# A decoder layer on one core: keys ahead of the query rotation, two units ahead of the scan, products in another order, residual in the accumulators, last tile by chunks

## The chip, the core and the metric

The kernel runs on one core of a Trainium2 chip. The core has TensorE (PE, the matmuls; PEld is its weight load), VectorE (DVE), ScalarE (ACT), GpSimd (POOL) and SyncE (SP), on whose queue nearly all DMAs are issued. The metric is the device time of one execution in microseconds (us), lower is better, as a median of runs.

## The reference

One step of a hybrid decoder layer in fp32: sliding-window attention with sinks and a Mamba-2 scan, both from one input projection and gated into one residual, then a squared-ReLU MLP. 1024 prompt positions and 8 single decode tokens go through the same weights (the kernel holds them as 1032 columns, T). Model width 1024, 16 query heads and 4 key heads of 64, window 128, 32 scan heads of 64 in 4 groups with a state of 128, MLP width 4096.

```python
def hybrid_layer(x, pos, ...):
    h = rms_norm(x, norm_mix)
    q, k, v, z, xbc, dt_raw, gates = jnp.split(h @ w_in, IN_SPLITS, axis=-1)
    q = rope(rms_norm(q.reshape(b, t, N_HEADS, HEAD_DIM), q_norm), pos)
    k = rope(rms_norm(k.reshape(b, t, KV_HEADS, HEAD_DIM), k_norm), pos)
    ...
    xc, conv_state = causal_conv(xbc, conv_prev, conv_w, conv_b)
    xs, Bm, Cm = jnp.split(xc, ...)
    y, h_fin = ssd_scan(xs_h, dt, A, Bm, Cm, ssm_h0)
    y = (y + d_skip[:, None] * xs_h).reshape(b, t, D_INNER)
    o_ssm = rms_norm(y * jax.nn.silu(z), ssm_norm)
    g_attn, g_ssm = jnp.split(jax.nn.sigmoid(gates), 2, axis=-1)
    mixed = g_attn * (o_attn @ w_attn_o) + g_ssm * (o_ssm @ w_ssm_o)
    x = x + mixed @ w_out
    u = rms_norm(x, norm_mlp) @ w_up
    x = x + jnp.square(jax.nn.relu(u)) @ w_down
    return x, new_k, new_v, conv_state, h_fin
```

## The kernel before

Activations lie with features on the partitions and the 1032 positions along the free side, in chunks (CH) of 384, 384 and 264 columns. Each fp32 matrix is kept as a high and a low fp32r part: `split` (L134) is a copy on ACT (L135) and a subtraction on DVE (L136). A product is three matmuls per 128 rows of K, high by high, high by low, low by high (`mm3`, L154).

**The stages.** Norm of the input and keys and values, until about 95 us; attention, mixed with matmuls of the input projection for other outputs, until 430; the scan, mixed with more of them, until 1080; output projections and the gate, until 1460; the MLP's up product, until 1827; its down product, until the end.

**Units.** Work of the input projection that something else can be laid over stands in a list of jobs, one for each 128 output columns. `unit` (L212) takes one chunk of a job: 24 matmuls and the eviction from PSUM. A conv job (L613) is three units; when its third is evicted, ACT makes the first tap (L629), DVE three more (L632 and L633 for each), ACT a Silu (L634), and the tile is an operand of the scan.

**Order.** From L838 to L1251 PE runs its instructions in the order of the code; within L840 to L852 ACT and DVE do too. Elsewhere a list scheduler orders each engine's queue.

**Attention's start.** L841 and L842 scale the rotary tables, `q_unit` (L692) makes a query tile and loads its shifted copy sw by DMA, `q_rot` (L709) rotates it on DVE and POOL and splits it into E and Od, `q_norm` (L729) makes its scales, `k_tiles` (L676) transposes the keys ktm (written at L443) on PE and splits them into KHH (ACT) and KLL (DVE). The scores (sc, L766) need E, Od, KHH and KLL.

**The scan.** Four groups g of eight chunks c. `front` (L1078) makes the decay matrix w (ACT), transposes B and x on PE (L1099) and scales them; `back` (L1112) makes state and output; its results go through yt (L1140) on DVE. `decode_unit` (L1036) is the decode token's part, without PE. PSUM for this comes from `bank` (L1075). 18 units run ahead of group 0 (L1154); then n of them are spread over the eight chunks of a group, half of a chunk's ahead of its back (L1171 to L1179).

**MLP up.** Each pair of 128x128 blocks is made by a scheme of seven products with sums of weight blocks and of input blocks (L1556 to L1610) for 16 pairs m. The first two products of the first eight m are made earlier and stored (p1). `prod` (L1412) is 12 matmuls of 258 columns, twice for a product (s = 0, 1). X and Y are two pairs of PSUM banks; u2, u3 and c21 are sums on DVE. `pair_loads` (L1548) loads the weights of the next m, `emit_u` (L1438) makes relu and square on ACT and writes u to DRAM. The inputs' sums are held in x23, x14 and x22 (L1495 to L1498).

**MLP down.** Eight passes e over the 4096 rows, each of four tiles of u that `load_ups` (L1537) loads by chunks (ld) and splits; within a pass eight output tiles n of three chunks, 12 matmuls each; DVE adds the sum into dacc (L1655). In pass 0 the other addend is the residual, loaded by chunk (xr, L1651). In the last pass `emit_y` (L1621) transposes tile n - 1 behind tile n, evicts it in two halves (yo, two buffers, L1629) and stores it; tile 7 comes last (L1659).

## Time and profile before

| | |
|---|---|
| median of 3 runs | 2214.3 us (2213.69 to 2218.34) |
| the profiled execution | 2215.28 us, its span 2213.5 us |
| busy: PE, DVE, ACT, POOL | 97%, 61%, 45%, 14% of the span |
| mean granted clock of PE | 0.992 of full speed |
| moved by DMA | 258.6 MB, mean 117 GB/s |

The profile is of one execution. Busy is the time in which an engine works on an instruction; the rest is waiting, for another engine, a DMA or nothing that the profile shows. The granted clock is 1 at 2.4 GHz and 0.5 at 1.2 GHz.

### The profile page before, as it was taken

How to read it: one execution, taken by the hardware profiler on the slowest of the kernel's cores; microseconds unless marked ns; L12 is line 12 of the kernel's file. 1: busy time of each engine (PE TensorE's matmuls, PEld its weight loads, DVE VectorE, ACT ScalarE, POOL GpSimd, SP SyncE). 2: the span in 40 equal slices, each digit the busy share in tenths (PEclk: the TensorE clock that was granted, in tenths of full speed). 3: DMA queues.
4: the chain of work that ended last, by engine and by line, in shares of the span. 5: the costliest groups of instructions: out<-in, count | busy, mean ns of one | idle time of the engine just before them, and what ended most of it. 6: DMA issues, size and time to landing. Idle time of an engine off the chain costs nothing.

```text
span 2213.5 us, 38986 instructions
## 1 busy us (share of the span) xinstructions
PE 2148.3 (97%) x14860; PEld 2045.0 (92%) x14860; DVE 1347.7 (61%) x2900; ACT 1006.4 (45%) x2040; POOL 318.7 (14%) x394
## 2 busy tenths in 40 slices
PE   7989999998999999999999999999999999999998
PEld 7989999997888898877999999999999998999998
DVE  6788787247756766677254867468665544544442
ACT  4265555235657656567353333336545542211112
POOL 1222222001213222223200003230000000000000
PEclk9999999999999999999999999999999999999999
DMA  5222233312324224133475766656443345332222
GB/s 189 81 77 67 74 101 91 98 54 64 91 68 127 61 80 122 42 84 103 117 228 175 237 195 190 185 169 190 139 120 101 113 129 176 111 100 87 86 71 79
DMA packets 341889, 258.64 MB, mean 117 GB/s; under 512 B 30864, under 2 KB 326503, under 8 KB 341661
## 3 DMA queue, kind: packets, MB, share of 16 engines
q1 hardware_dynamic: 340085, 254.87, 38.5%
q8 instruction: 117, 1.92, 0.4%
q10 hardware_dynamic: 1616, 1.28, 0.2%
q14 instruction: 71, 0.58, 0.1%
HBM read 180.26 MB, written 73.67 MB: 115 GB/s over the span
## 4 chain that ended last, share of the span: by engine, by line
PE 80%; DVE 9%; DMA 5%; ACT 4%; issue 2%; SPq 1%; POOL 0%; DVEq 0%; ACTq 0%; POOLq 0%
PE mm L158 14%; PE mm L159 14%; PE mm L160 14%; PE dn L158 5%; PE dn L160 5%; PE dn L159 5%; PE mm L1418 2%; PE mm L1419 2%; PE mm L1420 2%; PE dn L1418 2%; PE dn L1420 2%; PE dn L1419 2%; DMA bcb<-bc_d 2%; PE psy L1132 1%; PE psi L1125 1%
## 5 line engine op out<-in xcount | busy, mean ns | idle before, releaser
L158 PE MATMUL mm<-hT_h,wh 128*128 128x384 f32 (+1 forms) x1536 | 501.4, 326 | 1.1 <-ACT spill L239 1.1
L160 PE MATMUL mm<-hT_h,wl 128*128 128x384 f32 (+1 forms) x1536 | 492.1, 320 | 0.0
L159 PE MATMUL mm<-hT_l,wh 128*128 128x384 f32 (+1 forms) x1536 | 491.9, 320 | 0.0
L158 PEld LDWEIGHTS mm<-hT_h,wh 128*128 128x128 f32 x1536 | 290.3, 189 | 14.0 <-issue 12.1
L135 ACT ACTIVATE wh<-wraw 128x1024 fp32r<-128x1024 f32 (+1 forms) x157 | 160.3, 1023 | 296.5 <-PE dn L159 181.7
L159 PEld LDWEIGHTS mm<-hT_l,wh 128*128 128x128 f32 x1536 | 290.1, 189 | 0.0
L160 PEld LDWEIGHTS mm<-hT_h,wl 128*128 128x128 f32 x1536 | 289.6, 189 | 0.0
L158 PE MATMUL mm<-oh,wh 128*128 128x384 f32 (+2 forms) x832 | 257.2, 309 | 1.3 <-ACT pr L1306 1.1
L160 PE MATMUL mm<-oh,wl 128*128 128x384 f32 (+2 forms) x832 | 256.0, 308 | 1.4 <-DVE wl L136 1.4
L136 DVE TENSOR_TENSOR wl<-wraw,wh 128x1024 fp32r<-128x1024 f32 (+1 forms) x157 | 187.1, 1194 | 115.2 <-ACT wh L135 114.2
L159 PE MATMUL mm<-ol,wh 128*128 128x384 f32 (+2 forms) x832 | 256.8, 309 | 0.0
L1655 DVE TENSOR_TENSOR dacc<-dacc,dn 128x384 f32<-128x384 f32 x168 | 85.6, 510 | 150.4 <-PE dn L160 150.4
L158 PEld LDWEIGHTS mm<-oh,wh 128*128 128x128 f32 x832 | 156.6, 188 | 2.4 <-ACT pr L1306 1.5
L160 PEld LDWEIGHTS mm<-oh,wl 128*128 128x128 f32 x832 | 156.8, 188 | 1.6 <-DVE wl L136 1.6
L159 PEld LDWEIGHTS mm<-ol,wh 128*128 128x128 f32 x832 | 156.4, 188 | 0.0
L632 DVE SCALAR_TENSOR_TENSOR xc<-raw,prm,xc 128x1024 f32<-128x1024 f32 x72 | 93.5, 1299 | 7.0 <-ACT xc L629 6.9
L784 ACT ACTIVATE cm<-cm,nm,rq 128x128 f32<-128x128 f32 x128 | 61.7, 483 | 54.2 <-DVE nm L780 54.2
L1322 POOL TENSOR_TENSOR gr<-gr,rs 128x384 f32<-128x384 f32 (+1 forms) x24 | 29.2, 1218 | 272.1 <-ACT gr L1321 266.3
L1047 DVE SCALAR_TENSOR_TENSOR s<-s,dap,uu 128x128 f32<-128x128 f32 x128 | 47.5, 398 | 33.7 <-ACT uu L1046 33.6
L1046 ACT ACTIVATE uu<-bcb,dtp 128x128 f32<-128x128 f32 x128 | 42.4, 391 | 50.5 <-DMA bcb<-bc_d 49.5
L1284 DVE STREAM_TRANSPOSE xo<-xt 32x256 f32<-32x256 f32 x128 | 55.8, 436 | 8.1 <-DMA xT_d<-xo 3.9
L624 ACT ACTIVATE raw<-mm 128x384 f32<-128x384 f32 (+1 forms) x72 | 32.1, 447 | 60.6 <-PE mm L160 60.5
(821 smaller groups left out, 5366.8 us busy)
## 6 DMA issues: line engine op xcount, KB each, us to landing
wraw<-in_w_in SPq DMA_DIRECT2D x64, 512.0 KB
u_d<-u SPq DMA_DIRECT2D x64, 258.0 KB
wraw<-in_w_down SPq DMA_DIRECT2D x32, 512.0 KB
wraw<-in_w_up SPq DMA_DIRECT2D x27, 512.0 KB
ld<-u_d SPq DMA_DIRECT2D x56, 192.0 KB
xt<-in_x_prompt SPq DMA_DIRECT2D x16, 512.0 KB
s<-in_state_ssm SPq DMA_DIRECT2D x32, 256.0 KB
out_ssm_sample<-s SPq DMA_DIRECT2D x32, 256.0 KB
```

The source lines that it names most:

```text
L135: first = S.activation(h, src, AF.Copy)
L136: second[:] = [V.tensor_tensor(l, src, h.bitcast(F32), ALU.subtract)]
L158: TE.matmul(ps, lhsT=a, rhs=h, start=k == 0, stop=False)
L159: TE.matmul(ps, lhsT=a, rhs=l, start=False, stop=False)
L160: TE.matmul(ps, lhsT=b, rhs=h, start=False, stop=k == kt - 1)
L632: V.scalar_tensor_tensor(out[:, :NP], raw[:, k:k + NP], wk, out[:, :NP], ALU.mult, ALU.add)
L784: S.activation(cm[:, h, :], cm[:, h, :], AF.Exp, bias=nm[:, h:h + 1], scale=rq[:, j, h:h + 1], accum_out=sm[:, h:h + 1])
L1284: V.transpose(xo[32 * j:32 * j + 32, :, 32 * i:32 * i + 32], xb[32 * i:32 * i + 32, :, j, :])
L1418: TE.matmul(ps, lhsT=a, rhs=h, start=first and k == 0, stop=False, skip_group_check=True)
L1419: TE.matmul(ps, lhsT=a, rhs=l, start=False, stop=False, skip_group_check=True)
L1420: TE.matmul(ps, lhsT=b, rhs=h, start=False, stop=k == 3, skip_group_check=True)
L1655: V.tensor_tensor(ac[:, cs], prev, ps[:, :cn], ALU.add)
```

## The change

Five edits. (A) `k_tiles(0)` is called ahead of the first `q_rot` and not behind the second unit. (B) 20 units and not 18 stand ahead of the first scan, and 19, not 21, are spread over its group 0. (C) The seven products come in another order: into the banks X vt2, X vt3, Y vt1, X vt4, Y v22 before, and X vt2, Y vt1, X vt3, Y v22, X vt4 now; the pairs of input sums are placed in tiles accordingly. (D) The residual is loaded into the accumulators dacc by eight loads of a whole tile, `residual(n)`, four ahead of the first weights of pass 0 in the code and four behind; the chunk loads xr go, and all passes add alike. (E) `emit_y` can do a part of a tile; tile n - 1 is emitted behind the first chunk of tile n, and tile 7 by chunks of three, three and two blocks.

```diff
@@ -842,12 +842,12 @@
...
             q_unit(0, 0, 0)
             q_unit(0, 0, 1)
+            k_tiles(0)
             q_rot(0, 0, 0)
             unit(ahead=False)
             q_norm(0, 0)
             q_rot(0, 0, 1)
             unit(ahead=False)
-            k_tiles(0)
             unit(ahead=False)
             prefetch()
         blocks = [(kv, b) for kv in range(NKV) for b in range(NB)]
@@ -1151,7 +1151,7 @@
         rows(1)
...
-        unit(18)
+        unit(20)
         for g in range(NG):
...
@@ -1168,7 +1168,7 @@
...
-            n = (21, 27, 27, 9)[g]
+            n = (19, 27, 27, 9)[g]
...
@@ -1492,10 +1492,10 @@
     def xpair(i):
         return tuple(xv.tile([P, T], F32R, tag=f"x{i}{t}", name=f"x{i}{t}") for t in "hl")
 
-    x23 = [xpair(q) for q in range(4)]
-    x14 = [xpair(4 + q) for q in range(4)]
+    x21 = [xpair(q) for q in range(4)]
+    x34 = [xpair(4 + q) for q in range(4)]
     x22 = [tuple(xv.tile([P, HT], F32R, name=f"v{q}{t}") for t in "hl") for q in range(4)]
-    vt2, vt3, vt1, vt4, v22 = chunk_of(x23, 0), chunk_of(x23, HT), chunk_of(x14, 0), chunk_of(x14, HT), chunk_of(x22, 0)
+    vt2, vt1, vt3, vt4, v22 = chunk_of(x21, 0), chunk_of(x21, HT), chunk_of(x34, 0), chunk_of(x34, HT), chunk_of(x22, 0)
...
@@ -1513,24 +1513,24 @@
         V.tensor_tensor(b11_, b12_, b11_, ALU.subtract)
         t2 = mp.tile([P, HT], F32, tag="sa", name="t2")
...
-        split(x23[q][0][:, H0], x23[q][1][:, H0], t2)
+        split(x21[q][0][:, H0], x21[q][1][:, H0], t2)
...
     for q in range(4):
-        split(x23[q][0][:, H1], x23[q][1][:, H1], xrow[q][:, H1])
+        split(x21[q][0][:, H1], x21[q][1][:, H1], xrow[q][:, H0])
     early(5)
     wa[6] = w_first(6)
     for q in range(4):
-        split(x14[q][0][:, H0], x14[q][1][:, H0], xrow[q][:, H0])
+        split(x34[q][0][:, H0], x34[q][1][:, H0], xrow[q][:, H1])
     early(6)
     wa[7] = w_first(7)
     for q in range(4):
-        split(x14[q][0][:, H1], x14[q][1][:, H1], xrow[q + 4][:, H0])
+        split(x22[q][0][:], x22[q][1][:], xrow[q + 4][:, H1])
     early(7)
     for q in range(4):
-        split(x22[q][0][:], x22[q][1][:], xrow[q + 4][:, H1])
+        split(x34[q][0][:, H1], x34[q][1][:, H1], xrow[q + 4][:, H0])
 
...
@@ -1565,12 +1565,12 @@
         V.tensor_tensor(s2, s1, a11, ALU.subtract)
         w2, w3, w4 = wslot(), wslot(), wslot()
         split(w2[0][:, 0:4], w2[1][:, 0:4], s2)
+        split(w2[0][:, 4:8], w2[1][:, 4:8], s1)
         V.tensor_tensor(a21, a11, a21, ALU.subtract)
-        split(w2[0][:, 4:8], w2[1][:, 4:8], a21)
-        split(w3[0][:, 0:4], w3[1][:, 0:4], s1)
-        split(w3[0][:, 4:8], w3[1][:, 4:8], a22)
+        split(w3[0][:, 0:4], w3[1][:, 0:4], a21)
         V.tensor_tensor(a12, a12, s2, ALU.subtract)
-        split(w4[0][:, 0:4], w4[1][:, 0:4], a12)
+        split(w3[0][:, 4:8], w3[1][:, 4:8], a12)
+        split(w4[0][:, 0:4], w4[1][:, 0:4], a22)
 
...
@@ -1579,7 +1579,7 @@
         X = [bank(s) for s in range(2)]
         Y = [bank(s) for s in range(2)]
         pc = [p1[:, s * HC:(s + 1) * HC] for s in range(2)]
-        u2, u3 = [], []
+        u2, t5 = [], []
         for s in range(2):
             prod(X[s], w2, 0, vt2(s), True)
             u2.append(mp.tile([P, HC], F32, tag="u2", name="u2"))
@@ -1587,47 +1587,56 @@
         if m >= FP:
             second_product(m, w1, A)
         for s in range(2):
-            prod(X[s], w2, 4, vt3(s), False)
-            u3.append(mp.tile([P, HC], F32, tag="u3", name="u3"))
-            V.tensor_tensor(u3[s], X[s], pc[s], ALU.add)
+            prod(Y[s], w2, 4, vt1(s), True)
+            t5.append(mp.tile([P, HC], F32, tag="u3", name="t5"))
+            V.tensor_tensor(t5[s], Y[s], pc[s], ALU.add)
         if m == NM - 1:
             load_ups(0, lambda: p1t("ld"), HT)
         u = u_tile()
         for s in range(2):
-            prod(Y[s], w3, 0, vt1(s), True)
-            V.tensor_tensor(u3[s], u3[s], Y[s], ALU.add)
-            emit_u(2 * m + 1, 1, u, s, u3[s])
+            prod(X[s], w3, 0, vt3(s), False)
+            V.tensor_tensor(t5[s], X[s], t5[s], ALU.add)
+            emit_u(2 * m + 1, 1, u, s, t5[s])
         u = u_tile()
         for s in range(2):
-            prod(X[s], w3, 4, vt4(s), False)
+            prod(Y[s], w3, 4, v22(s), False)
+            V.tensor_tensor(u2[s], Y[s], u2[s], ALU.add)
+            emit_u(2 * m, 1, u, s, u2[s])
+        u = u_tile()
+        for s in range(2):
+            prod(X[s], w4, 0, vt4(s), False)
             c21 = mp.tile([P, HC], F32, tag="ca", name="c21")
             V.tensor_tensor(c21, X[s], pc[s], ALU.add)
             emit_u(2 * m + 1, 0, u, s, c21)
-        u = u_tile()
-        for s in range(2):
-            prod(Y[s], w4, 0, v22(s), False)
-            V.tensor_tensor(u2[s], u2[s], Y[s], ALU.add)
-            emit_u(2 * m, 1, u, s, u2[s])
     mst.close()
     lst.close()
 
 
     dap_ = ctx.enter_context(pool("dap", 1))
     yp = ctx.enter_context(pool("yp", 2))
-    accs = [dap_.tile([P, T], F32, name=f"dacc{n}") for n in range(8)]
+    accs = {n: dap_.tile([P, T], F32, name=f"dacc{n}") for n in (4, 5, 6, 7, 0, 1, 2, 3)}
+
+    def residual(n):
+        DQ.dma_start(accs[n], x2_d[n])
+
     FE = 4
     NE = 32 // FE
 
-    def emit_y(n):
+    def emit_y(n, c0=0, cn=T):
+
         ac = accs[n]
         ns = slice(n * P, (n + 1) * P)
+        b0, b1 = c0 // P, min((c0 + cn) // P, NB)
         ps = ptr.tile([P, NB, P], F32, tag="tr", name="psy2")
-        for tb in range(NB):
+        for tb in range(b0, b1):
             TE.transpose(ps[:, tb, :], ac[:, tb * P:(tb + 1) * P], ident)
-        for hf in range(2):
+        for t0 in range(b0, b1, 4):
+            t1 = min(t0 + 4, b1)
             yo = yp.tile([P, 4, P], F32, tag="yo", name="yo")
-            S.activation(yo, ps[:, 4 * hf:4 * hf + 4], AF.Copy)
-            DQ.dma_start(O["y_prompt"][0, 512 * hf:512 * hf + 512, ns].rearrange("(b p) n -> p b n", p=P), yo)
+            S.activation(yo[:, 0:t1 - t0], ps[:, t0:t1], AF.Copy)
+            DQ.dma_start(O["y_prompt"][0, t0 * P:t1 * P, ns].rearrange("(b p) n -> p b n", p=P), yo[:, 0:t1 - t0])
+        if c0 + cn < T:
+            return
         ps = pdn.tile([P, 512], F32, tag="dn", name="dnd")
         TE.transpose(ps[:ND, :P], ac[:, NP:T], ident)
         yd = yp.tile([ND, P], F32, tag="yd", name="yd")
@@ -1635,7 +1644,13 @@
         DQ.dma_start(O["y_sample"][:, 0, ns], yd)
 
     for e in range(NE):
+        if e == 0:
+            for n in range(4):
+                residual(n)
         w0 = load_w(w_dn, 0, k0=e * FE, kt=FE, ncol=256)
+        if e == 0:
+            for n in range(4, 8):
+                residual(n)
         if e + 1 < NE:
             load_ups(e + 1, lambda: yp.tile([P, 384], F32, tag="ld", name="ld", bufs=4), 384)
         uh = lambda k: ups[e][k][0]
@@ -1646,17 +1661,14 @@
                 ac = accs[n]
                 for c0, cn in CH:
                     cs = slice(c0, c0 + cn)
-                    if e == 0:
-                        xr = yp.tile([P, 384], F32, tag="xr", name="xr")
-                        DQ.dma_start(xr[:, :cn], x2_d[n, :, cs])
                     ps = pdn.tile([P, 512], F32, tag="dn", name="dn")
                     mm3(ps[:, :cn], wh, wl, uh, ul, FE, c0, cn, n0=(n % 2) * P)
-                    prev = xr[:, :cn] if e == 0 else ac[:, cs]
-                    V.tensor_tensor(ac[:, cs], prev, ps[:, :cn], ALU.add)
-                if e == NE - 1:
-                    if n:
-                        emit_y(n - 1)
-    emit_y(7)
+                    V.tensor_tensor(ac[:, cs], ac[:, cs], ps[:, :cn], ALU.add)
+                    if e == NE - 1:
+                        if n and c0 == 0:
+                            emit_y(n - 1)
+                        if n == 7:
+                            emit_y(n, c0, cn)
```

**A.** DVE's queue at the start of attention, both pieces of the difference in which KLL (L689) is named; L841 and L842 are the table scales, L714 and L716 the rotation.

```order
 L841 TENSOR_SCALAR cosq<-cosq,sml 128x1032
 L842 TENSOR_SCALAR sinq<-sinq,sml 128x1032
+L689 TENSOR_TENSOR KLL<-pk,KHH 64x512 x4
 L714 TENSOR_TENSOR q<-q,cosq 128x384
 L716 TENSOR_TENSOR q<-q,sw 128x384
```

```order
 L714 TENSOR_TENSOR q<-q,cosq 128x384
 L716 TENSOR_TENSOR q<-q,sw 128x384
-L689 TENSOR_TENSOR KLL<-pk,KHH 64x512 x4
 L136 TENSOR_TENSOR wl<-wraw,wh 128x1024
 L773 COPY_PREDICATED cm<-maski,sc 128x512
```

The four subtractions of KLL moved from behind both rotations to the place ahead of the first.

**B.** ACT's queue around the first front of the scan, before: L624 evicts a unit, L629 and L634 begin and end the last conv tile that the front reads, L1092 and L1093 make the decay matrix.

```order
L624 ACTIVATE raw<-mm 128x384
L135 ACTIVATE wh<-wraw 128x1024
L624 ACTIVATE raw<-mm 128x264
L1092 ACTIVATE w<-pdf 128x512
L629 ACTIVATE xc<-raw,prm 128x1032
L1092 ACTIVATE w<-pdf 128x512
L1104 ACTIVATE bt<-pcb 128x128
L1093 ACT_TABLE_LOAD
L1093 ACTIVATE w<-w 128x1024
L634 ACT_TABLE_LOAD
L634 ACTIVATE xc<-xc 128x1032
```

The same place now:

```order
L624 ACTIVATE raw<-mm 128x384
L135 ACTIVATE wh<-wraw 128x1024
L624 ACTIVATE raw<-mm 128x264
L629 ACTIVATE xc<-raw,prm 128x1032
L624 ACTIVATE raw<-mm 128x384
L634 ACTIVATE xc<-xc 128x1032
L624 ACTIVATE raw<-mm 128x384
L1092 ACTIVATE w<-pdf 128x512 x2
L1104 ACTIVATE bt<-pcb 128x128
L1093 ACT_TABLE_LOAD
L1093 ACTIVATE w<-w 128x1024
```

The evictions of two more units stand between the last conv tile's steps, and its Silu stands ahead of the front's work.

**D.** SP's queue from the end of MLP up into the down product, before: L1444 writes u, L1545 loads u (the 516 wide for pass 0, the 384 wide for pass 1), L1651 loads the residual by chunk, L143 loads weights.

```order
L1444 DMA u_d_76<-u_20322 128x516
L1545 DMA ld_20548<-u_d_76 128x384
L1545 DMA ld_20404<-u_d_76 128x516
L1545 DMA ld_20408<-u_d_76 128x516
L1545 DMA ld_20412<-u_d_76 128x516
L1545 DMA ld_20416<-u_d_76 128x516
L1545 DMA ld_20552<-u_d_76 128x384
L1545 DMA ld_20556<-u_d_76 128x384
L1545 DMA ld_20560<-u_d_76 128x384
L1651 DMA xr_20596<-x2_d_75 128x384
L1444 DMA u_d_76<-u_20420 128x516
L1651 DMA xr_20612<-x2_d_75 128x384
```

Now, from the second write of u on (four loads of 516 columns and the load of dacc0 stand between it and the write above it):

```order
L1444 DMA u_d_76<-u_20420 128x516
L1620 DMA dacc1_20531<-x2_d_75 128x1032
L1620 DMA dacc2_20532<-x2_d_75 128x1032
L1620 DMA dacc3_20533<-x2_d_75 128x1032
L1444 DMA u_d_76<-u_20452 128x516
L1444 DMA u_d_76<-u_20484 128x516
L1620 DMA dacc4_20526<-x2_d_75 128x1032
L1620 DMA dacc5_20527<-x2_d_75 128x1032
L1620 DMA dacc6_20528<-x2_d_75 128x1032
L1620 DMA dacc7_20529<-x2_d_75 128x1032
L1545 DMA ld_20556<-u_d_76 128x384
L1545 DMA ld_20560<-u_d_76 128x384
```

The first loads of u for pass 1 stood ahead of the second write of u, among the writes; they stand now behind the last write and behind all eight residual loads.

On DVE, the same place, now: L136 splits weights (wl) and u (x4l to x7l), L1666 adds into the accumulators (L1655 before).

```order
L136 TENSOR_TENSOR wl<-wraw,wh 128x1024
L1666 TENSOR_TENSOR dacc_20530<-dacc_20530,dn 128x384 x2
L1666 TENSOR_TENSOR dacc_20530<-dacc_20530,dn 128x264
L1666 TENSOR_TENSOR dacc_20531<-dacc_20531,dn 128x384 x2
L1666 TENSOR_TENSOR dacc_20531<-dacc_20531,dn 128x264
L136 TENSOR_TENSOR x4l<-ld,x4h 128x384
L136 TENSOR_TENSOR x5l<-ld,x5h 128x384
L1666 TENSOR_TENSOR dacc_20532<-dacc_20532,dn 128x384
```

The six adds of the first two tiles stand ahead of x4l; before, the first add stood behind x4l and x5l.

## Rows read from the trace of the kernel before

**Rows 1.** The page, busy us (share of the span) and instructions of each engine.

```profile
PE 2148.3 (97%) x14860; PEld 2045.0 (92%) x14860; DVE 1347.7 (61%) x2900; ACT 1006.4 (45%) x2040; POOL 318.7 (14%) x394
```

**Rows 2.** Who PE waited for: us in total, times, longest us.

```profile
PE pxt L1099 <- ACT xc L634: 6.7, 1, 6.7
...
PE mm L1418 <- DVE u L1586: 4.9, 4, 1.8
PE dn L158 <- DVE dacc L1655: 3.4, 1, 3.4
PE sc L766 <- ACT KHH L687: 2.9, 1, 2.9
PE pxt L1099 <- DVE yt L1140: 2.6, 1, 2.6
```

**Rows 3.** Stretches: length, busy PE PEld DVE ACT POOL, PEclk, DMA share, GB/s.

```profile
514.00:518.70 4.70, 0.00 (x1) 0.00 (x1) 4.57 (x7) 4.61 (x4) 1.07 (x2) 0.50 0.50 138
518.70:523.90 5.20, 5.20 (x17) 4.14 (x18) 4.18 (x15) 4.61 (x9) 1.53 (x3) 0.50 0.14 40
550.00:658.00 108.00, 103.74 (x687) 90.89 (x686) 72.39 (x170) 63.90 (x102) 20.29 (x31) 0.98 0.29 83
1540.00:1660.00 120.00, 113.11 (x932) 111.93 (x931) 75.87 (x153) 58.35 (x132) 0.00 (x0) 1.00 0.46 142
...
1826.00:1846.30 20.30, 15.16 (x95) 14.19 (x93) 12.98 (x24) 11.14 (x24) 0.00 (x0) 0.97 0.71 230
1832.00:1836.00 4.00, 4.00 (x28) 4.00 (x28) 2.62 (x5) 0.89 (x1) 0.00 (x0) 1.00 1.00 325
1846.30:1852.00 5.70, 5.70 (x21) 5.70 (x22) 1.39 (x3) 0.00 (x0) 0.00 (x0) 0.52 0.77 250
```

**Rows 4.** Timeline at attention's start, ACT, DVE, POOL: start, us, instruction [idle before <-releaser].

```profile
94.36 0.49 ACT L702 ACTIVATE q<-mm 128x384 f32<-128x384 f32 x1 [3.33 <-PE mm L160]
...
96.31 0.96 DVE L443 TENSOR_TENSOR ktm<-kb,rk 128x768 f32<-128x768 f32 x1
...
104.35 0.76 DVE L842 TENSOR_SCALAR sinq<-sinq,sml 128x1032 f32<-128x1032 f32 x1 [1.11 <-DMA sinq<-in_sin_fm]
...
106.75 0.56 DVE L716 TENSOR_TENSOR q<-q,sw 128x384 f32<-128x384 f32 x1 [0.91 <-POOL sw L715]
...
116.20 2.79 DVE L689 TENSOR_TENSOR KLL<-pk,KHH 64x512 fp32r<-64x512 f32 x4 [2.72 <-ACT KHH L687]
...
115.18 0.99 POOL L722 TENSOR_TENSOR Od<-q,Od 64x384 fp32r<-64x384 f32 x1
```

**Rows 5.** Timeline of ACT, the conv job before the last one.

```profile
499.94 0.37 ACT L624 ACTIVATE raw<-mm 128x264 f32<-128x264 f32 x1
...
505.89 1.07 ACT L634 ACTIVATE xc<-xc 128x1032 f32<-128x1032 f32 x1 [2.03 <-DVE xc L633]
```

**Rows 6.** The page's groups: count | busy us, mean ns | idle before, its releaser.

```profile
L632 DVE SCALAR_TENSOR_TENSOR xc<-raw,prm,xc 128x1024 f32<-128x1024 f32 x72 | 93.5, 1299 | 7.0 <-ACT xc L629 6.9
```

**Rows 7.** Timeline of DVE in MLP up.

```profile
1559.74 0.69 DVE L1564 TENSOR_TENSOR s<-wraw 128x512 f32<-128x512 f32 x1 [2.88 <-DMA wraw<-in_w_up]
```

**Rows 8.** Timeline of SP and DVE at the start of MLP down.

```profile
1831.14 0.32 SPq L1444 DMA_DIRECT2D u_d<-u  x1
...
1842.92 0.43 DVE L136 TENSOR_TENSOR x5l<-ld,x5h 128x264 fp32r<-128x264 f32 x1 [2.34 <-ACT x5h L135]
...
1845.70 0.88 DVE L1655 TENSOR_TENSOR dacc<-xr,dn 128x384 f32<-128x384 f32 x2
```

**Rows 9.** The page, what the DMAs moved in the whole span.

```profile
DMA packets 341889, 258.64 MB, mean 117 GB/s; under 512 B 30864, under 2 KB 326503, under 8 KB 341661
```

**Rows 10.** Timeline of ACT at the end.

```profile
2208.72 0.60 ACT L1629 ACTIVATE yo<-psy 128x512 f32<-128x512 f32 x1 [1.70 <-DMA out_y_prompt<-yo]
```

**Rows 11.** The chain that ended last, in order of time: start, us, what.

```profile
2202.52 0.18 PE dn L160
...
2204.57 0.12 PE dn L160
```

## Prediction

> **What bounds the kernel now.** I read the page's busy table first: TensorE (PE) is busy 2148.3 of 2213.5 us [rows 1], so the whole kernel is one PE queue with 65 us of holes in it, and an edit can win only holes and the slow-clock time behind them. Next the table of who PE waited for: the reader is to see five of its entries, each at a place that the change touches [rows 2]. They make 20.5 us. Then the stretches around those places with their granted clock [rows 3], because a hole is followed by matmuls at half clock. Last the timelines of DVE, ACT and SP ahead of each hole, for what ended last there [rows 4, 5, 7, 8]. PE runs the order that the code gives, so a hole closes only if other matmuls stand ahead of the wait, or what is waited for comes earlier. A matmul of 384 columns takes 0.18 us, one of 264 takes 0.12 [rows 11]; a unit of 24 takes 24 x 0.18 = 4.3 us.
>
> **A, keys ahead of the query rotation: about 1.5.** The scores waited 2.9 us for the key halves KHH [rows 2], since the key transposes stood behind two units. The last operand was KLL, done at 116.20 + 2.79 = 118.99 [rows 4]. Now the transposes come right behind the second query unit, which PE leaves when ACT starts to evict it, at 94.36. They read ktm, which DVE ends at 96.31 + 0.96 = 97.27: a new wait of up to 2.9 us, with the two units behind it. That wait falls ahead of the same scores, so it is not lost twice; what counts is when the scores have all operands. KLL's 2.79 us now stand on DVE between sinq (ends 105.11) and the first rotation multiply. They push the multiply from 105.28 to 107.90, by 2.6; the 0.91 that DVE waited there for POOL is covered by it, so the rotation chain comes 1.7 later, and its last product Od moves from 115.18 + 0.99 = 116.17 to 117.9 [rows 4]. The scores are then ready at 117.9 and not at 119.0: 1.1 gained, and something of the half-clock stretch behind the old hole. I take 1.5. Bounds: -1, if the rotation chain slips by all of 2.6 and the wait for ktm cools the clock, to +2.5, nearly the whole old wait.
>
> **B, two units more ahead of the first scan: about 10.** The hole of 6.7 us is the first transposes of the scan waiting for the Silu of the last conv tile [rows 2]. That tile's last unit stood directly ahead. The conv job before shows how long this takes: its eviction ends at 499.94 + 0.37 = 500.31 and its Silu at 505.89 + 1.07 = 506.96, 6.65 us later [rows 5]. Two units are 8.6 us of PE work, so Silu comes in time and the hole is gone: 6.7. In the old hole the clock fell to 0.50, and PE then worked 5.2 us at 0.50 [rows 3]; at full clock this takes 2.6, so 2.6 more. The second hole, 2.6 us for yt [rows 2], arose since DVE was held by three conv steps of 1.3 us [rows 6]; with 19 units spread over eight chunks and not 21, two units now stand between that step and its reader, so I count it as closed. The stretch behind has a granted clock of 0.98 over 108 us [rows 3]; that is 2.2 us lost, of which I give this hole 1.5. Together 13.4.
>
> What is given back: the second chunk's front now follows the first at once and needs banks that ACT must empty first, about one eviction, 0.5. And the unit counts per chunk go from 2,3,2,3,3,2,3,3 to 2,2,3,2,2,3,2,3: twice two neighbouring chunks have only two units each, so one conv job's 3 x 1.3 = 3.9 us of DVE work [rows 6] can stand against a unit less of cover. On the mean DVE is not the bound, 72.4 of 108 us [rows 3], but the old yt hole shows that a burst can be. I take 3 of the 3.9. 13.4 - 0.5 - 3 = 9.9. Bounds: 5, which is 6.7 + 2.6 - 0.5 - 3.9 with nothing for the second hole, to 13.4. The two units aren't extra work: the same units run later otherwise.
>
> On the clock, the rows show 4.7 us at 0.50 without a PE instruction to speak of, then 5.2 us at 0.50 with PE busy, and I charge only the second. The Trainium skill ("TensorE: Matmul & The Clock Gate", section Terms) gives the penalty as the throttled time times (1 - K/N), which charges all of it: 9.9 x 0.5 = 5.0 and not 2.6. By that rule B would be worth 2.4 more; no row shows this, since an engine that has nothing to do loses nothing by its clock.
>
> **C, the seven products in another order: about 6.** In the stretch of the first eight m, PE is idle 120 - 113.11 = 6.89 us at full clock [rows 3], 4.9 of it for the add that empties X (L1586) [rows 2]. Before, PE accumulates into X again right after one product of 1.45 us (12 matmuls of 258 columns at 0.12), and the add stands on DVE behind two weight sums, the first of which waits 2.88 us for its weights [rows 7]. In the new order the banks alternate X, Y, X, Y, X, so each bank has one more product's pair between its add and its next use, 4.4 us and not 1.45. The longest of the waits was 1.8 [rows 2], which fits in the new 2.9 of slack. Counts of adds and splits are unchanged, and the operand tiles hold other halves at equal cost. What is late next is the weights themselves: where the DMA is late by more than the slack, the first product waits. I take 6 of 6.89; bounds 4 (a part of the 4.9 stays) to 7.
>
> **D, residual loaded into the accumulators: about 4.5.** It removes 24 loads of a chunk (L1651) and adds 8 loads of a whole row block, 528 KB each: the same 4.23 MB. DVE's adds no longer need a load of their own. The old hole: DVE waits 2.34 us for an ld chunk (x5l), so the add into dacc starts only at 1845.70 [rows 8], PE waits 3.4 [rows 2] and then works 5.7 us at clock 0.52 [rows 3], 2.9 lost. Sum 6.3. After, six adds stand on DVE ahead of x4l, so PE has n = 0 and 1 and three banks of n = 2, 3 x 5.8 = 17.4 us from about 1828, until 1845.6, before it feels a late ld.
>
> The new cost is on SP's queue: four dacc loads stand between the last write of u (issued at 1831.14 [rows 8]) and the ld loads, and two or three are still under way there. So the first ld lands behind some 3 MB. At 325 GB/s with the DMA engines full [rows 3] that is 9 us, 1841, and nothing waits. At the 230 of the whole stretch [rows 3] it is 13 us plus the split, 1845 to 1846, just at the edge, and the second ld chunks behind it can cost 0 to 3. I take 230 with a loss of 1.8. Bounds: at +8 the smaller waits at the start of the stage go too; at -4 three chunks are late in turn and the clock falls once more.
>
> **E, last tile by chunks: about 1.5.** The last matmul ends at 2204.57 + 0.12 = 2204.69 [rows 11]; what follows is add, eight transposes, two evictions and the store, with 1.70 us of ACT waiting for a yo buffer [rows 10]. Now the first six blocks leave while PE still works, and two blocks remain. The transposes of six blocks move ahead of the last matmuls and cost them nothing in sum. The wait for a yo buffer halves, 0.8, and 0.7 of transposes and adds goes. Bounds 0 to 2.5.
>
> **Sum.** 1.5 + 10 + 6 + 4.5 + 1.5 = 23.5. The profiled execution took 2215.3 (span 2213.5 and 1.8 around it), so 2191.8; the median of the runs is 2214.3, 1.0 lower, so **2191**.
>
> **The rivals.**
> R1, the scan gives back: the conv bursts on DVE take 5 more of B (it ends at its lower bound), the ld loads eat D's 4.5, and C loses 1.5 to late weights. For it: the yt hole, and the DMA engines at full share [rows 3]; against it: DVE's 67% there. Gain 23.5 - 11 = 12.5, so 2202, between 2199 and 2208.
>
> R2, slower: the residual loads crowd out what the down stage needs. By the end of its first pass (8 x 5.8 = 46 us) it must have 4.23 MB of residual, 2.1 MB of u and 2.1 MB of weights, 8.4 MB. A, B, C and E give 19; the loss passes that when the 8.4 MB take over 65 us, which is below 130 GB/s. At the 117 GB/s of the run's mean [rows 9] they take 72: 26 lost, 7 net, 2221. Against it: 230 to 325 GB/s were moved in this very place.
>
> R3, the holes only move: DVE or ACT is late at the next place each time (the ktm wait in A, fronts in B, the first product in C). Then little beyond E and a part of the clock is won, some 3 us: 2211.
>
> R4, the whole half-clock stretch counts: what PE waits for in B's hole comes in part from work that the slow clock has made late, so the 4.7 idle us at 0.50 [rows 3] shrink too, by half: 2.4 more, 2188. For it: nothing but the clock's value; against it: the hole ends on ACT's Silu, which isn't PE's. (It is the skill's rule above.)
>
> **How the numbers follow.** Forecast 2191: 0.57, own range 2181 (all upper bounds together, 2.5 + 13.4 + 7 + 8 + 2.5 = 33.4) to 2199, where R1's begins. R1 0.25, R2 0.06, R3 0.08, R4 0.04. The range 2181 to 2207 holds the forecast, R4 and nearly all of R1, and leaves out R2 and R3. About 0.2% (4.4 us) is what can be told from no change here. Faster: 0.57 + 0.25 + 0.04 = 0.86. Same: R3 at 2211 is within 0.2%, with a little of it beyond, 0.07; slower: R2 and the worst of R3, 0.07.
>
> **What would show it.** A: the scores' wait is on POOL's Od, and a wait of 2 to 3 us for ktm stands near 95. B: no wait for xc over 1 us before the first scan, no half clock behind it; if the bursts cost, waits for yt, xdt or cbm rise in the first group. C: the wait for L1586's add gone. D: no PE wait for dacc near 1843; if it fails, DVE waits for ld after 1846 and PE for its banks. E: the span ends under 7 us after the last matmul of 384 or 264 columns. I am wrong if PE's idle time stays over 50 us, or if one of the new waits is longer than the one that it replaces.

## The result, and the profile after

The changed kernel takes 2187.8 us (median of 4 runs, 2187.05 to 2188.17) against 2213.99 before (2212.43 to 2218.34): 0.9878 of the time, 95% interval 0.9861 to 0.9895, 26.2 us less. The profiled execution has a span of 2186.5 where before had 2213.5. The page's first part, which answers to [rows 1]:

```profile
PE 2139.3 (98%) x14860; PEld 2035.8 (93%) x14860; DVE 1344.4 (61%) x2900; ACT 1003.6 (46%) x2039; POOL 319.7 (15%) x394
```

With as many matmuls as before PE is idle 47.2 us, not 65.2 (18.0 less), and busy 2139.3, not 2148.3 (9.0 less; for the greater part these are matmuls at half clock that now run at full). The two make the 27.0 by which the spans differ. Who PE waited for, as in [rows 2] (us in total, times, longest):

```profile
PE pk L683 <- DVE ktm L443: 3.1, 1, 3.1
PE mm L158 <- DVE gr L1271: 2.1, 3, 1.6
...
PE pdf L1091 <- ACT w L1092: 1.5, 1, 1.5
...
PE sc L766 <- POOL Od L722: 0.6, 1, 0.6
PE psy L1632 <- DVE dacc L1666: 0.6, 1, 0.6
PE dn L1418 <- DVE u L1586: 0.6, 1, 0.6
...
PE mm L1418 <- DVE u L1586: 0.3, 1, 0.3
```

The waits of [rows 2] for xc, yt, KHH and dacc (L1655) are gone. Those for u (L1586) are 0.3 and 0.6, where before had 4.9 [rows 2] and, into the second bank, this one:

```profile
PE dn L1418 <- DVE u L1586: 1.1, 1, 1.1
```

The first row is the new wait for ktm. The places of [rows 3] (length, busy PE PEld DVE ACT POOL, PEclk, DMA share, GB/s): the first front of the scan, the scan's first group, MLP up, and 20 us from 2 us ahead of the first down matmul:

```profile
511.40:523.90 12.50, 12.50 (x81) 11.17 (x80) 8.18 (x12) 8.03 (x12) 2.73 (x6) 1.00 0.19 53
536.40:644.40 108.00, 106.38 (x719) 91.98 (x718) 79.66 (x206) 65.36 (x114) 22.55 (x33) 1.00 0.35 99
...
1528.00:1646.00 118.00, 116.21 (x957) 114.98 (x956) 78.31 (x157) 60.86 (x137) 0.00 (x0) 1.00 0.49 150
1808.60:1828.60 20.00, 20.00 (x132) 19.82 (x131) 11.98 (x22) 8.54 (x17) 0.00 (x0) 1.00 0.89 312
```

The reader is to see PE full and the clock at 1.00 in the first and the last, where [rows 3] had a hole and 0.50 to 0.52, and 312 GB/s in the last, where the old stretch had 230.

**Where the 27.0 us came from**, by the time of one matmul at the end of each stage in the two traces, and, in the same manner, for the single edits (us less than the profile of before). The attention column ends at the first decode score, the scan's at the last output of group 1, the second of its four groups. The projections' column holds the scan's other two groups too, and ends at the first product of MLP up; MLP up's ends at its last product, and MLP down's at the first matmul of its last pass, some 60 us ahead of the end:

| kernel | attention | scan | projections | MLP up | MLP down | end | span |
|---|---|---|---|---|---|---|---|
| all edits | 0.2 | 14.8 | -3.0 | 4.3 | 8.3 | 2.4 | 27.0 |
| all edits, again | 1.5 | 13.5 | -0.3 | 5.1 | 8.5 | 2.4 | 30.6 |
| A alone | 0.6 | 2.2 | -3.0 | 0.5 | 3.0 | -0.1 | 3.3 |
| B alone | -2.8 | 15.0 | 0.4 | -0.6 | 2.8 | -0.1 | 14.8 |
| C alone | -0.5 | -0.1 | -1.7 | 4.0 | 3.1 | -0.1 | 4.7 |
| D alone | 0.2 | -0.5 | -1.8 | -0.1 | 8.3 | 0.0 | 6.1 |
| E alone | -1.3 | 0.1 | -1.7 | 0.0 | 2.6 | 2.4 | 2.2 |

A column of kernels that don't touch its stage shows what one profile is worth: the profile of before was about 2.9 us slow in MLP down (3.0, 2.8, 3.1, 2.6 without D) and about 1.6 fast in the projections; in the scan A alone, which changes nothing there, was 2.2 faster.

### The profile page after: what moved, and what is told of

Same layout as the page of the kernel before. It is cut to its first block, busy times and chain, and to the rows that moved or that the text cites. A ratio compares the mean times of both kernels' runs of the same rounds, so it can differ in the third digit from the quotient of the medians.

```text
span 2186.5 us, 38961 instructions
## 1 busy us (share of the span) xinstructions
PE 2139.3 (98%) x14860; PEld 2035.8 (93%) x14860; DVE 1344.4 (61%) x2900; ACT 1003.6 (46%) x2039; POOL 319.7 (15%) x394
## 4 chain that ended last, share of the span: by engine, by line
PE 80%; DVE 8%; DMA 7%; ACT 2%; issue 2%; SPq 1%; POOL 0%; ACTq 0%; DVEq 0%; POOLq 0%
PE mm L158 13%; PE mm L159 13%; PE mm L160 13%; PE dn L158 6%; PE dn L160 6%; PE dn L159 6%; PE mm L1418 2%; PE mm L1419 2%; PE mm L1420 2%; PE dn L1418 2%; PE dn L1420 2%; PE dn L1419 2%; PE psy L1132 1%; PE psi L1125 1%; PE pst L1128 1%
## 5 line engine op out<-in xcount | busy, mean ns | idle before, releaser
L136 DVE TENSOR_TENSOR wl<-wraw,wh 128x1024 fp32r<-128x1024 f32 (+1 forms) x156 | 185.9, 1193 | 130.6 <-ACT wh L135 129.8
L1666 DVE TENSOR_TENSOR dacc<-dacc,dn 128x384 f32<-128x384 f32 (+1 forms) x192 | 97.7, 510 | 169.6 <-PE dn L160 169.4
L624 ACT ACTIVATE raw<-mm 128x384 f32<-128x384 f32 (+1 forms) x72 | 32.2, 447 | 61.6 <-PE mm L160 61.6
```

The costliest lines, as they stand in the source:

```text
L136: second[:] = [V.tensor_tensor(l, src, h.bitcast(F32), ALU.subtract)]
L1666: V.tensor_tensor(ac[:, cs], ac[:, cs], ps[:, :cn], ALU.add)
```

## The experiments

**One edit at a time.** Each takes one of the five edits of the diff and leaves the rest as before. B, as the shortest:

```diff
-        unit(18)
+        unit(20)
...
-            n = (21, 27, 27, 9)[g]
+            n = (19, 27, 27, 9)[g]
```

> Edit A alone. Theory: the wait for KHH (2.9 us) is swapped for one for ktm of about 3 us, and the scores then wait for the rotated query; how much is won hangs on when the sine table lands, 104.35 before and 106.13 with all edits, since KLL stands behind its scaling. With the table at 104.4: scores end 0.8 to 1.5 us earlier than before, 2213.2 in all; with the table at 106: nothing. Rival, the swap is exact and the table has no part: scores end within 0.3 of before whenever the table comes.

> Edit B alone. Theory: the gain is that of the holes of the first group, whatever stands elsewhere: 14 to 15 us at the last matmul of group 1's output, so about 2199.5 in all. The 2.6 us that the projections between 1125 and 1225 gave back with all edits are a matter of when loads land, not of B: gone here, or of another size. Rival: they belong to B's shift in time: then 12 at the end, 2202.

> Edit C alone. Theory: the order of products wins 4.3 us between the first product of the loop and the last, as it did with all edits, 2210 in all, and no wait for L1586 over 0.6 is left. Rival: part of the 4.3 came from the shift of the whole stage or from D's loads: under 3 alone, 2211.5 or more.

> Edit D alone. Theory: wide loads move the bytes at about 300 GB/s, the u chunks of pass 1 land before PE's cover ends, and the down stage wins 8.3 us as with all edits: 2206 in all. Rival: C's order (the up stage ending on another product) let the u writes and so the loads start earlier; alone D wins the 4.5 that was forecast or less, 2209.5 or more.

> Edit E alone. Theory: the last tile by chunks wins 2.4 us between the first down matmul of the last pass and the end, as it did with all edits, of which about 0.8 is given by the yo buffers of which no third transfer has to be waited for. Rival: with all edits part of it came from elsewhere (D took xr's buffers out of the pool): 1.5 or less alone.

Measured (median, ratio to before with interval; before took 2214.65 beside the first four and 2216.71 beside E): A 2211.9, 0.999 (0.9979 to 1.0001); B 2202.66, 0.994 (0.992 to 0.9959); C 2210.01, 0.9974 (0.9964 to 0.9985); D 2209.2, 0.9972 (0.9961 to 0.9982); E, one execution, 2213.04. By stage B, C, D and E each win alone, within 0.3 us, what they win in the first profile of all edits; its second profile differs from the first by 1.3 in the scan and 0.8 in MLP up. The totals add up as well: 2.8 + 12.0 + 4.6 + 5.5 and the 2.4 of E's stage are 27.3, and all edits won 26.2. So nothing here shows that the edits help or hinder one another, as far as these medians tell; the totals of A and E alone don't resolve their gains.

Two totals missed. B's, 2202.66, is the time of its rival, not the 2199.5 of the theory. The rival's reason isn't in B's profile, whose projections gave nothing back (0.4); that execution lost 2.8 in attention, which B does not touch, and for the median of the four nothing more is known. D's, 2209.2, is 3.2 over the 2206 expected, which had taken over the 8.3 of the first profile. Of these, 2.9 belong to the profile of before: 8.3 - 2.9 = 5.4, and the medians say 2214.65 - 2209.2 = 5.45. The rival's reason, C's order, is out all the same, since D alone wins 8.3 in that stage as all edits do.

A needs its own measure. The table scaling (L842) waits for a DMA whose landing differs from execution to execution; with A KLL stands right behind it (here in A alone):

```profile
105.61 0.76 DVE L842 TENSOR_SCALAR sinq<-sinq,sml 128x1032 f32<-128x1032 f32 x1 [2.23 <-DMA sinq<-in_sin_fm]
106.28 2.79 DVE L689 TENSOR_TENSOR KLL<-pk,KHH 64x512 fp32r<-64x512 f32 x4
109.10 0.56 DVE L714 TENSOR_TENSOR q<-q,cosq 128x384 f32<-128x384 f32 x1
```

From the start of that scaling to the end of the first scores it is 14.7 to 15.1 us in the five profiles without A, and 13.3 to 13.7 in the eight with it: A wins 1.5. The scaling itself starts between 104.35 [rows 4] and 106.13 in these, and that hid it: 104.35 + 14.94 = 119.29 before, 106.13 + 13.28 = 119.41 with all edits. The rival, an exact swap in which the table has no part, is out. But counted from the start of the execution A wins less: the first scores end at 119.6 in the mean of the five and at 118.8 in that of the eight, 0.8 earlier, since the scaling starts at 104.7 and at 105.4 in the mean. Whether A itself makes the table land later is not shown.

**19 and 22 units ahead of the first scan**, all other edits kept:

```diff
-        unit(20)
+        unit(19)
...
-            n = (19, 27, 27, 9)[g]
+            n = (20, 27, 27, 9)[g]
```

> All edits, but 19 units ahead of the first scan and 20 spread over its group. Theory (the Silu comes about 7 us after the last unit it needs, and a unit covers 4.3 of it): a wait of pxt for xc of 2.3 to 3 us comes back ahead of the first scan and up to 2 us of slow clock behind it; the end of group 1 comes 2 to 5 us later than with 20. Rival: one unit is enough and the second only makes the bursts in group 0: no wait over 1 us, group 1 ends within 1 us of 20 or earlier.

> All edits, but 22 units ahead of the first scan and 17 spread. Theory (what binds is only the cover ahead of the first scan, and with 20 it is there; DVE has room): the end of group 1 within 1 us of 20 units, no new wait over 1.5. Rival, conv bursts on DVE against thinner cover (what 3 us were set aside for in the prediction): waits for yt, xdt or w come up in group 0 and it ends 2 to 5 us later.

With 19 the scan wins 5.3 and not 14.8, 9.5 less where 2 to 5 were expected: PE waits 4.8 us for xc, where 2.3 to 3 were expected, and is busy 4.7 longer, with matmuls at half clock. The execution takes 2195.25. ACT's timeline shows why the wait is so long, and the line below it DVE's last step for that tile:

```profile
515.16 1.08 ACT L1092 ACTIVATE w<-pdf 128x512 f32<-128x512 f32 x2
516.26 1.28 ACT L1093 ACT_TABLE_LOAD   x1
517.56 1.06 ACT L1093 ACTIVATE w<-w 128x1024 f32<-128x1024 f32 x1
518.63 1.28 ACT L634 ACT_TABLE_LOAD   x1
519.93 1.06 ACT L634 ACTIVATE xc<-xc 128x1032 f32<-128x1032 f32 x1
516.89 0.22 DVE L633 SCALAR_TENSOR_TENSOR xc<-raw,prm,xc 128x8 f32<-128x8 f32 x1
```

The Silu (L634) stands behind the front's Exp (L1093) and two table loads, 3.6 us, and starts 2.8 us after DVE is done (517.11). In the kernel before, ACT's queue has the same order, but it cost nothing: Exp and table loads were through when DVE was, and the Silu starts 0.14 us after DVE's last step (517.44):

```profile
517.22 0.22 DVE L633 SCALAR_TENSOR_TENSOR xc<-raw,prm,xc 128x8 f32<-128x8 f32 x1
517.58 1.06 ACT L634 ACTIVATE xc<-xc 128x1032 f32<-128x1032 f32 x1
```

With 20 the Silu comes ahead of the Exp, right after DVE's last step:

```profile
514.51 0.49 ACT L624 ACTIVATE raw<-mm 128x384 f32<-128x384 f32 x1 [1.75 <-PE mm L160]
517.04 1.07 ACT L634 ACTIVATE xc<-xc 128x1032 f32<-128x1032 f32 x1 [2.04 <-DVE xc L633]
```

So two units do two things: they cover the 7 us, and they bring the Silu ahead of the Exp in ACT's queue. With 22 the execution takes 2186.99; the scan wins 12.4, and PE's waits in the first group are these:

```profile
PE pdf L1091 <- ACT w L1092: 1.2, 1, 1.2
PE pcb L1095 <- DVE bcs L1161: 0.8, 1, 0.8
PE pxt L1099 <- DVE xdt L1107: 0.2, 1, 0.2
```

None is over 1.5, and none is for yt. But group 1 ends 2.0 us later than with 20 (the theory allowed 1), in the main by a half-clock stretch behind the wait near 641 that the first profile of all edits had not (more on that in the last section). What is new in waits, for bcs and xdt on DVE, comes to 1.0 where the prediction set 3 us aside for bursts, so the theory fits better than the rival, and its 1 us was too narrow for one profile.

**The residual by chunks, and more bytes**, all edits kept:

```diff
-        DQ.dma_start(accs[n], x2_d[n])
+        for c0, cn in CH:
+            DQ.dma_start(accs[n][:, c0:c0 + cn], x2_d[n, :, c0:c0 + cn])
```

```diff
         DQ.dma_start(accs[n], x2_d[n])
+        if n > 3:
+            DQ.dma_start(dap_.tile([P, T], F32, name=f"extra{n}"), x2_d[n])
```

> All edits, but each residual tile is loaded by three loads of a chunk, 24 in all, at the same place of the queue and with the same bytes. Theory (wide rows move faster: 312 GB/s over the first 20 us of the down stage with all edits, 230 before): the rate falls back towards 230 to 260 and the first u chunk of pass 1 is split 3 us later or more than with wide loads (12.8 us after the first down matmul there), close to the end of PE's cover at 17.4, so 0 to 3 us are lost. Rival: the rate is the same and it was the taking away of waits on DVE's queue that raised it: the split comes within 1 us of the same time and nothing is lost.

> All edits, and four more loads of a residual tile into tiles that nobody reads, 2.1 MB, between those of dacc 4 to 7 and the u chunks of pass 1. Theory (the u chunks land behind the bytes ahead of them): at about 310 GB/s the first split comes 6.8 us later, some 19.5 us after the first down matmul; PE's cover ends at 17.4, so PE waits 2 to 3.5 us there and loses up to 3 more by its clock. Rival: transfers share the engines and the u chunks aren't held back by bytes ahead: the split comes under 3 us later and PE does not wait.

The 20 us from 2 us ahead of the first down matmul, by chunks and then with more bytes:

```profile
1807.90:1827.90 20.00, 19.23 (x124) 18.70 (x123) 8.50 (x16) 6.84 (x15) 0.00 (x0) 1.00 0.89 284
```

```profile
1806.00:1826.00 20.00, 20.00 (x132) 19.82 (x131) 9.20 (x17) 4.91 (x11) 0.00 (x0) 1.00 0.96 365
```

A split is a copy on ACT (x4h) and a subtraction on DVE (x4l). The 12.8 us of the expectations are those of the copy. The first of pass 1 with all edits, by chunks, and with more bytes; the first down matmul starts at 1810.62, 1809.86 and 1808.02:

```profile
1823.40 0.53 ACT L135 ACTIVATE x4h<-ld 128x384 fp32r<-128x384 f32 x1 [10.17 <-DMA ld<-u_d]
1823.96 0.56 DVE L136 TENSOR_TENSOR x4l<-ld,x4h 128x384 fp32r<-128x384 f32 x1 [1.24 <-ACT x4h L135]
```

```profile
1826.06 0.53 ACT L135 ACTIVATE x4h<-ld 128x384 fp32r<-128x384 f32 x1 [13.00 <-DMA ld<-u_d]
1826.62 0.56 DVE L136 TENSOR_TENSOR x4l<-ld,x4h 128x384 fp32r<-128x384 f32 x1 [3.77 <-ACT x4h L135]
```

```profile
1825.69 0.53 ACT L135 ACTIVATE x4h<-ld 128x384 fp32r<-128x384 f32 x1 [15.06 <-DMA ld<-u_d]
1827.47 0.55 DVE L1668 TENSOR_TENSOR dacc<-dacc,dn 128x384 f32<-128x384 f32 x1 [1.68 <-PE dn L160]
1827.94 0.55 DVE L136 TENSOR_TENSOR x4l<-ld,x4h 128x384 fp32r<-128x384 f32 x1
```

By chunks the copy comes 16.2 us after the first down matmul and not 12.8 (the subtraction 16.8 and not 13.3), and MLP down wins 5.3 and not 8.3: 3.0 lost, the theory's side in time. Its reason, narrow rows, is not shown alone. The rate, of all traffic in those 20 us, fell to 284 and not to 260; and 24 loads take longer to issue than 8, so the loads of u left SP's queue 12.0 us after the first down matmul and not 6.3. SP's queue, with all edits and then by chunks:

```profile
1813.63 3.22 SPq L1620 DMA_DIRECT2D dacc<-x_d  x4
1816.90 2.02 SPq L1545 DMA_DIRECT2D ld<-u_d  x4
```

```profile
1813.45 8.35 SPq L1621 DMA_DIRECT2D dacc<-x_d  x13
1821.90 1.80 SPq L1545 DMA_DIRECT2D ld<-u_d  x4
```

No run tells the number of issues from the width of the rows.

With 2.1 MB more the copy comes 17.7 us after the first down matmul, 4.9 later than with all edits: more than the rival's 3, less than the theory's 6.8, at 365 GB/s. The subtraction comes only at 19.9, since it stands behind ten adds on DVE there, not six (the last of them is in the fence), and with four more adds done PE can go on longer. MLP down wins 7.4, where the kernels with the residual as in all edits win 7.6 to 8.5, so the 2 us or more of waiting did not come. How late u lands is one thing; what PE feels of it depends on how many adds stand ahead of the split on DVE.

**Another order at attention's start**, all edits kept, and the changed kernel again beside it:

```diff
+            q_unit(0, 0, 0)
+            q_unit(0, 0, 1)
+            unit(ahead=False)
+            k_tiles(0)
             V.tensor_scalar(cosq, cosq, sml[:, 0:1], None, ALU.mult)
             V.tensor_scalar(sinq, sinq, sml[:, 1:2], None, ALU.mult)
-            q_unit(0, 0, 0)
-            q_unit(0, 0, 1)
-            k_tiles(0)
             q_rot(0, 0, 0)
-            unit(ahead=False)
-            q_norm(0, 0)
             q_rot(0, 0, 1)
             unit(ahead=False)
+            q_norm(0, 0)
             unit(ahead=False)
```

> All edits, but at attention's start the key transposes stand behind the first unit, KLL ahead of the scaling of the two tables on DVE, and both query rotations ahead of the query norms. Theory (A won under 1 us since it swapped the wait for KHH for one for ktm, and put KLL ahead of the rotation on DVE, behind the late sine table): the 3.1 us wait for ktm is gone, KLL runs while DVE waits for the tables, the scores' operands are there at about 112.5 and the first scores end at 114 to 116, 3.5 to 5.5 earlier than with all edits; 2183.5 in all. Rival (the query path or the units' evictions bind there, whatever the order): the scores end within 1 us of 119.4 and a wait for E, Od or a spill takes the place.

> The changed kernel once more, on the same chip as the kernel with the other order at attention's start. Theory: 2187 to 2189; its stage from the last scan output to the first product of MLP up, 706.3 us in its first profile and 702.9 to 706.4 in the other kernels with the same instructions there, comes out anywhere in that spread. Rival: it belongs to the changed kernel and is 706 again within 0.3.

The other order takes 2184.71 (0.9856, 0.9836 to 0.9877), the changed kernel 2185.81 (0.9866, 0.9843 to 0.9889): no difference that these runs resolve. The changed kernel comes out a little under the 2187 to 2189 expected, and 30.9 us under the 2216.71 of before beside it, where the first runs gave 26.2. With the other order the wait for ktm is gone, and from the sine table to the end of the scores it is 10.8 us and not 13.3, but the scores end at 117.7: not at 114 to 116, and not within 1 us of 119.4 as the rival had it. A wait of the rival's kind took the place. The code does not set POOL's order there, the second query's product (L715) stands behind the first one's two subtractions, and the scores wait 2.84 us for it; without that wait they would have ended at 114.8. The table was late too (its scaling starts at 106.89).

```profile
110.47 1.01 POOL L721 TENSOR_TENSOR E<-q,E 64x384 fp32r<-64x384 f32 x1 [1.29 <-ACT E L719]
111.55 1.00 POOL L722 TENSOR_TENSOR Od<-q,Od 64x384 fp32r<-64x384 f32 x1
112.63 0.99 POOL L715 TENSOR_TENSOR sw<-sw,sinq 128x384 f32<-128x384 f32 x1
```

**Three buffers for the gate's chunks**, all edits kept (`chunk("gr", 3)` for `chunk("gr")`):

> All edits, and three buffers in place of two for the gate's chunks (gr) in the output projections. Theory (the 3.5 us of spread from the scan's end to MLP up come from the loop of gate load, sigmoid, product and store, in which a load of about 4 us stands against 4.2 us of matmuls): no wait for L1271, and the stage takes 703 or less. Rival: the spread comes from elsewhere (the row statistics, the operand loads): 704 to 706 and waits of another kind.

The stage takes 704.5 us, and PE still waits for L1271:

```profile
PE mm L158 <- DVE gr L1271: 2.1, 1, 2.1
```

The third buffer does not take the wait away, so the theory falls. The changed kernel again had 703.7 in that stage where its first profile had 706.3: the 3 us given back there are no property of the change. What makes the spread stays open.

## Why the prediction was right

The forecast was 2191, 23.3 us less; measured 2187.8, 26.2 less. It was right in kind at all five places, and its sizes err both ways. By stage, B, D and E came out 4.8, 3.8 and 0.9 over the forecast, A and C 1.3 and 1.7 under, and the projections, which no edit touches, lost 3.0. That the sums, 23.5 and 27.0, lie close is in part luck.

- **A, 1.5 forecast, 1.5 measured** against the sine table's landing, 0.8 from the start of the execution. The steps held: a wait for ktm in place of that for KHH, KLL pushing the rotation, the scores waiting last for Od. That they "are then ready at 117.9" held only for a table at 104.35, a landing that the prediction took as fixed. By one of its own signs A failed: the wait for ktm, 3.1, is longer than the 2.9 that it replaces. That cost little, since it falls ahead of the same scores, as the prediction had said.
- **B, 10 forecast, 14.8 and 15.0 measured in the first profiles**, above its bound of 13.4; the seven profiles with 20 units give 13.2 to 15.4, and the medians of B alone 12.0. The holes were read rightly: PE's idle time in that stage fell by 9.3, which is 6.7 + 2.6. Two terms were mis-sized. What is given back, 3.5, did not come: no wait for yt, xdt or cbm in the first group. And PE's busy time fell by 5.5, where 2.6 + 1.5 were counted for the clock (the stage before, and with all edits below). The margin was thinner than the prediction knew: with one unit the Silu falls behind the Exp and two table loads, and the wait is 4.8 where 6.65 [rows 5] less a unit would leave 2.4.

```profile
413.63:789.89 376.26, 364.07 (x2413) 330.04 (x2412) 229.79 (x503) 207.95 (x331) 71.36 (x109) 0.98 0.28 78
```

```profile
413.46:774.90 361.44, 358.60 (x2412) 325.42 (x2412) 226.94 (x503) 205.05 (x329) 72.06 (x109) 1.00 0.29 81
```

- **C, 6 forecast, 4.0 to 6.2 measured** (4.3 in the first profile, 5.1 in the mean of the nine that have it). The add's wait went as worked out. What came instead are small waits for p, t and u, 2.4 us in MLP up; 0.7 of them, for p, lie in the products made ahead of the loop, where the prediction took the new places of the input sums to cost nothing.
- **D, 4.5 forecast, 8.3 measured against the profile of before, 5.4 against kernels without it.** Against the profile of before, two terms were mis-sized. The rate: 230 was taken from the old stretch, 312 came, so u was split 12.8 to 13.3 us after the first down matmul and not at 17 to 18, and the 1.8 set aside was not lost. And two smaller waits at the stage's start, 1.1 for wh and 0.6 for wl, went as well; the prediction had them in its upper bound alone. The 2.9 that the kernels without D don't bear out are in part the clock: A alone waits 3.9 us there for dacc and C alone 2.8, with no stretch at half clock behind, where the profile of before has 3.4 and 5.7 us at 0.52 [rows 2, 3].
- **E, 1.5 forecast, 2.4 measured.** The wait for a yo buffer did not halve, it is 1.84 us, but it lies at the first part, beside matmuls; the last eviction waits for no buffer:

```profile
2180.54 0.49 ACT L1636 ACTIVATE yo<-psy 128x384 f32<-128x384 f32 x1 [1.84 <-DMA out_y_prompt<-yo]
...
2183.22 0.36 ACT L1636 ACTIVATE yo<-psy 128x256 f32<-128x256 f32 x1
```

Of the rivals, R1 asked for bursts in the scan and losses at the ld loads: neither came; even with 17 units spread DVE's new waits are 1.0, and 2.1 MB more cost 0.9. R2 asked for under 130 GB/s over the first down pass: 204 were moved with all edits. R3 is out by PE's idle time, 18.0 us less. R4, the half-clock stretch counted whole, forecast 2188, nearest to what was measured, and that is luck: its 2.4 more were to come from idle time, and PE's idle time in the scan fell by 9.3, which the two holes already are. What made B larger are the terms named above. The clock says the same: its mean rose from 0.992 to 0.999, which counted whole is (0.008 x 2213.5) - (0.001 x 2186.5), some 15 us, while PE's busy time fell by 9.0. (Counting it whole is the rule of the Trainium skill, "TensorE: Matmul & The Clock Gate", section Terms. The trace does not agree: 15 by the rule, 9.0 measured.)

## What to carry to other kernels

A wait of an in-order engine is closed by work put ahead of it, but count what the helper engine does first: a Silu that fell behind another function and two table loads came 2.8 us late, and the second unit of cover, 4.3 us of matmuls, brought 9.5. Eight whole-row loads ahead of a stage cost little here, where the adds that need nothing else stand ahead of the late splits; 24 narrow ones cost 3.0 more. And one profile's stage is good to 2 or 3 us: kernels that leave a stage alone are its controls, and a time that hangs on a DMA is measured from that DMA's landing.

## What the runs showed that was not expected

Whether the clock falls behind a hole of 1.2 to 1.6 us did not go by the hole's length. The wait of pdf for w near 641 was 1.5 in all edits and 1.5 in the residual by chunks; the granted clock of the 6 us or so that begin just ahead of it was 1.00 in the first and 0.86 in the second, where 3.4 us right behind it ran at 0.51:

```profile
640.00:646.50 6.50, 4.88 (x29) 3.43 (x28) 2.40 (x7) 4.22 (x8) 1.50 (x2) 1.00 0.41 105
```

```profile
639.50:645.50 6.00, 4.33 (x23) 3.38 (x23) 2.65 (x8) 4.58 (x9) 1.50 (x2) 0.86 0.34 93
643.98:647.38 3.40, 3.40 (x12) 3.40 (x12) 2.06 (x4) 3.39 (x7) 0.20 (x1) 0.51 0.02 5
```

That is 1.7 us of difference between executions, and it parts the gains of B: of the seven profiles with 20 units the three with that stretch have 13.2 to 13.5, the four without it 14.8 to 15.4. The wait for ktm does the same: 3.1 us both in all edits and in A alone, and behind it

```profile
98.50:102.00 3.50, 3.50 (x22) 3.50 (x21) 0.00 (x0) 1.18 (x2) 0.00 (x0) 1.00 0.59 174
```

```profile
98.50:102.00 3.50, 3.50 (x13) 3.50 (x12) 0.00 (x0) 1.14 (x2) 0.00 (x0) 0.53 0.65 206
```

There it cost next to nothing, since the scores wait for Od in either. And with the same 4.23 MB of residual at the same place of the queue, all traffic of those 20 us was 312 GB/s with its rows of 4128 bytes and 284 with rows of 1536 and 1056, with the DMA engines busy 0.89 in both; the later issue of the loads behind it may be part of that difference.
